# The weights' low part: an ACT negation and an accumulating DMA in place of DVE's subtraction

## Chip, cores and metric

One core of one Trainium2 chip runs the kernel. The metric is the device time of one execution in microseconds, the median of several runs. The work is in float32; the large products are done as float32r matmuls on split operands (below).

## The reference

Two transformer-like blocks are applied to 512 tokens of 1024 features. Cut to the dense products, which take most of the time:

```python
def first_block(x, p, ...):
    h = rms_norm(x, norm1_g)
    z = h @ w_in                     # 1024 -> 2304 columns, for four mixers
    x = x + concat(mixers(z)) @ w_out
    hf = causal_dwconv(rms_norm(x, norm2_g) @ w_up, ...)
    gt, val = split(hf)
    x = x + (gelu(gt) * val) @ w_down          # d_ff = 2816
    x = x + (p @ w_pe) * sigmoid(rms_norm(x, norm3_g) @ w_pg)
    return rms_norm(x, final_g)

def hybrid_layer(x, ...):            # the second block: two of these
    proj = (_rms(x) * norm1_g) @ w_in          # attention, RWKV, retention, gates
    mixed = g0 * (attention @ w_attn_o) + g1 * (rwkv @ w_rwkv_o) + g2 * (retention @ w_ret_o)
    x = x + mixed @ w_out
    h2 = _rms(x) * norm2_g
    return x + (silu(h2 @ w_ffn_gate) * (h2 @ w_ffn_up)) @ w_ffn_down    # d_ff = 2816
```

## The kernel before

Features lie on the 128 partitions and the 512 tokens along the free axis, so an activation is 8 tiles of 128 x 512. The weights come from DRAM in chunks of 128 x 1024 (512 KB): one output tile of 128 columns with its 8 k tiles of 128. There are 400 chunks: 138 of w_in (18 in the first block, 60 in each layer of the second), 44 of w_up, 24 of w_down, 24 of w_out, 8 of w_pg, 2 of w_pe, and in the two layers 88 of the gate and up weights, 48 of w_ffn_down, and 8 each of w_rwkv_o, w_attn_o and w_ret_o. The down products have 22 k tiles, in chunks of 8, 7 and 7.

Full precision comes from splitting. Each activation x is a pair (xh, xl) of float32r tiles whose sum is x, and each weight chunk is made into such a pair on the chip. `fetch` (L111) has SP load the raw chunk into one of three wraw buffers. `chunk` (L117) then lets ACT cast it to float32r (whi, L125), and DVE subtract that from the raw chunk (wlo, L126); whi and wlo have two buffers each. `mac` (L129) adds three products for every k tile, in this order, and PE works through its instructions in their order:

```python
self.nc.tensor.matmul(ps, hi[:, c], xh, start=first and k == 0, stop=False)          # L135
self.nc.tensor.matmul(ps, hi[:, c], xl, start=False, stop=False)                     # L136
self.nc.tensor.matmul(ps, lo[:, c], xh, start=False, stop=last and k == n - 1)       # L137
```

So a tile is 24 matmuls of 128 x 512, and wlo is wanted by the third of them. whi is free again when L136 of the last k tile has read it.

The stages follow each other: the first block's mixers, its w_up and w_down products (`ffn1`), the gate with w_pg; then for each of two layers the RWKV mixer, attention and retention, `combine` (L1319, which holds a chunk of w_attn_o and one of w_ret_o at once and uses each for two output tiles), w_out, and `ffn2` (L1342: gate and up tiles in turn, with DVE's L1350 and L1354, ACT's L1351 and the split L165, POOL's L1352; then the down product). In the mixers, dense tiles wait in a queue and are let in between the steps of the recurrences. POOL has some 280 instructions, single additions and multiplications such as L220 (the sum of squares for the norms) and L1352, and issues no DMA. SP issues nearly all of the DMAs.

The order of each engine's instructions comes from a scheduler that takes dependencies and priorities; fetch, cast and subtraction are raised by 300 places. On an engine the instructions run strictly in that order, and an instruction that waits holds up all that are behind it.

Of the kernel before, what the change touches and what calls it, by code (L numbers as in the profile page):

```python
# [10 lines left out]
F32 = mybir.dt.float32  # L11
F32R = mybir.dt.float32r
I32 = mybir.dt.int32
U8 = mybir.dt.uint8
AF = mybir.ActivationFunctionType
ALU = mybir.AluOpType
# [4 lines left out]
P = 128  # L21
# [4 lines left out]
EPS = 1e-6  # L26
# [8 lines left out]
class Kern:  # L35
# [9 lines left out]
    # Dense tiles that nothing waits for yet are kept in a queue; the mixers let  # L45
    # some of them in between their own steps, so that the tensor engine has work.
# [64 lines left out]
    def fetch(self, src):  # L111
        raw = self.tile(self.wp, [P, 1024], "wraw", bufs=3)
        with self.tc.high_priority(offset=300):
            self.nc.sync.dma_start(raw[:, :src.shape[-1]], src)
        return raw

    def chunk(self, src):  # L117
        """One chunk of a weight: its float32 values, and their two parts."""
        nc = self.nc
        n = src.shape[-1]  # L120
        raw = self.early.popleft() if self.early else self.fetch(src)
        hi = self.tile(self.wp, [P, 1024], "whi", F32R)
        lo = self.tile(self.wp, [P, 1024], "wlo", F32R)
        with self.tc.high_priority(offset=300):
            nc.scalar.copy(hi[:, :n], raw[:, :n])  # L125
            nc.vector.tensor_tensor(lo[:, :n], raw[:, :n], hi[:, :n].bitcast(F32), ALU.subtract)  # L126
        return hi, lo

    def mac(self, ps, w, xs, first, last):  # L129
        """ps += w.T @ x over the k tiles in xs, in three passes."""  # L130
        hi, lo = w
        n = len(xs)
        for k, (xh, xl) in enumerate(xs):
            c = slice(k * P, (k + 1) * P)
            self.nc.tensor.matmul(ps, hi[:, c], xh, start=first and k == 0, stop=False)  # L135
            self.nc.tensor.matmul(ps, hi[:, c], xl, start=False, stop=False)  # L136
            self.nc.tensor.matmul(ps, lo[:, c], xh, start=False, stop=last and k == n - 1)  # L137

    def dense(self, wname, m, xs, kcuts=None):
        """M tile m of a weight applied to the k tiles xs (pairs of parts)."""  # L140
        src = self.io[wname]
        ps = self.tile(self.mm, [P, 512], "mm")
        kcuts = kcuts or [len(xs)]
        k0 = 0
        for i, kn in enumerate(kcuts):
            w = self.chunk(src[m, :, k0 * P:(k0 + kn) * P])
            self.mac(ps, w, xs[k0:k0 + kn], i == 0, i == len(kcuts) - 1)
            k0 += kn
        return ps

    def dense2(self, wname, xs, use):
        """A weight with 4 k tiles: two M tiles to a chunk; use(m, psum)."""
        src = self.io[wname]
        for j in range(src.shape[0]):
            hi, lo = self.chunk(src[j])
            for i in range(2):
                ps = self.tile(self.mm, [P, 512], "mm")
                o = slice(i * 512, (i + 1) * 512)
                self.mac(ps, (hi[:, o], lo[:, o]), xs, True, True)
                use(2 * j + i, ps)  # L160

    def split_into(self, hi, lo, src, scale=1.0):
        """Two float32r parts of src * scale: hi + lo is exact."""
# [13 lines left out]
    def rsqrt(self, v, n):  # L177
        """v ** -0.5 for a small [128, n] tile of positive values."""
# [12 lines left out]
    def bcast(self, col):  # L191
        """[128 tokens, 4] -> PSUM [128, 512]: each token's value down a column."""
# [5 lines left out]
    def bcast_heads(self, col):  # L198
        """[128 tokens, 4 blocks x 2 heads] -> PSUM [2 x 64 features, 512 tokens]."""
# [7 lines left out]
    def token_sum(self, acc, ps, col):  # L207
        """Sum over features of acc into column col + 4 b of ps."""
# [16 lines left out]
    def norm_scale(self, acc):  # L225
        """The broadcast 1 / rms of the tokens, as an SBUF tile."""
# [32 lines left out]
    def mixers1(self, c2, x, xg, rb, pe):  # L259
# [19 lines left out]
        # small parameters  # L279
# [16 lines left out]
        # columns, the longest mixer's first  # L296
# [30 lines left out]
        # p @ w_pe, halved for the gate that comes later  # L327
# [29 lines left out]
        # the order of the k tiles on the host: d, a, b, c  # L357
# [50 lines left out]
    def rglru_consts(self, tp):  # L408
        nc, V = self.nc, self.vec
        # 2 softplus(-lam): e = exp(-|lam|), log1p(e) by the series of atanh  # L410
# [18 lines left out]
        # softplus(-lam) = max(-lam, 0) + 2 acc;  sp = twice that  # L429
# [73 lines left out]
    def hgrn2(self, zq, zf, zig, lvm, tp, yp):  # L503
        nc, V = self.nc, self.vec
        # lower bound: a softmax over the one layer, less its own first row
# [24 lines left out]
        # masked scores [s, t], one level of block size after another  # L530
        # (heads of one parity, a pair of windows: one PSUM bank)
# [57 lines left out]
        # values and decayed keys by token  # L589
# [10 lines left out]
        # states at the starts of the windows, block diagonal over pairs of heads  # L600
# [39 lines left out]
    def head_rms(self, dst, src, nh, tp, xi=None, xi2=None):  # L640
        """dst = src / rms over the last axis of [128, nh, 64] (src in PSUM); of src * xi, where given."""
# [13 lines left out]
    def ffn1(self, x, acc, xg, pe, xs_p):  # L655
# [28 lines left out]
        # the gate, and the two norms that follow it  # L684
# [3 lines left out]
        with tc.tile_pool(name="f1g", bufs=2) as gp:  # L688
# [14 lines left out]
            # y = a / rms(x4) with a = x4 * final_g; with v and w the means of the squares of  # L703
            # x4 and a, the norm of y on top comes to a * (w + EPS * (v + EPS)) ** -0.5
# [42 lines left out]
    def rwkv(self, c):  # L747
# [21 lines left out]
        # halves of parameters that go with tanh  # L769
# [33 lines left out]
        for p in range(4):  # L803
# [3 lines left out]
            # decays  # L807
# [13 lines left out]
            # in-context rate  # L821
# [4 lines left out]
            # keys  # L826
# [13 lines left out]
            # b, scaled; the order of the two halves of a chunk turns with its parity  # L840
# [8 lines left out]
            # bonus  # L849
# [6 lines left out]
            # values by token  # L856
# [6 lines left out]
            # scores  # L863
# [10 lines left out]
            # keys as they stand at the end of the chunk  # L874
# [6 lines left out]
    def rwkv_inverse(self, SC, kp):  # L881
        """The transposed inverses of I - A (64 x 64) in place of the A of SC."""
# [24 lines left out]
        # rows of the first diagonal block, for the block below it  # L907
# [28 lines left out]
    def rwkv_chain(self, SC, AR, BK, UV, end, gd, g2, kp):  # L936
# [29 lines left out]
        def ahead(c):  # L966
            """What a chunk needs apart from the state: decayed keys by token, products with the values."""
# [97 lines left out]
    def evac(self, dst, ps, scale=1.0):  # L1065
        """dst = ps * the tokens' 1 / rms (* scale)."""
# [42 lines left out]
    def att_proj(self, ap):  # L1109
# [10 lines left out]
        # keys and values  # L1120
# [17 lines left out]
        # queries: tile g has head g (of the first key head) over head 4 + g  # L1138
# [66 lines left out]
    def ret_proj(self, rp, rt):  # L1205
        """Queues the columns of the retention, and what is done to them one by one."""
# [48 lines left out]
    def retention(self, rp, op, q, k, vt, sg, cn):  # L1255
        nc, l = self.nc, self.l
        # the queries, keys and values, where the queue still has any
# [61 lines left out]
    def combine(self, oa, oc, mp):  # L1319
        """The gated sum of the three branches (twice it, halved in the split)."""  # L1320
# [56 lines left out]
def _w(a, per=1, cols=None, rows=None):  # L1377
    """[K, M] -> chunks [M tiles / per, 128, per * K tiles * 128], contiguous for a partition."""
# [13 lines left out]
def _col(v):  # L1392
    """[n * 128] -> [128, n]"""
    return np.ascontiguousarray(v.reshape(-1, P).T)


def _constants():
# [19 lines left out]
    # rotary angles and decays of the retention  # L1417
# [101 lines left out]
```

## Time and profile before

| | |
|---|---|
| median of 3 runs | 2668.3 us (2667.89 to 2669.66) |
| span of the profiled execution, from its first to its last instruction | 2666.0 us |
| what the median has beyond that span | 2.3 us |
| mean granted TensorE clock | 0.985 |
| busy: DVE, ACT, POOL | 1491.5, 893.7, 378.5 us |
| DRAM read, written | 244.42 MB, 31.72 MB |

The busy times are those of one execution, and an engine's share is an average over stages that differ. A time in a row of waits is the idle time of the engine at the left until the one at the right released it. Line numbers are those of the kernel before; in the changed kernel the lines of `mac` and all that is behind it stand two lower down (L135 becomes L137, L1352 becomes L1354).

### The profile page before, as it was taken

How to read it: one execution, taken by the hardware profiler on the slowest of the kernel's cores; microseconds unless marked ns; L12 is line 12 of the kernel's file. 1: busy time of each engine (PE TensorE's matmuls, PEld its weight loads, DVE VectorE, ACT ScalarE, POOL GpSimd, SP SyncE). 2: the span in 40 equal slices, each digit the busy share in tenths (PEclk: the TensorE clock that was granted, in tenths of full speed). 3: DMA queues.
4: the chain of work that ended last, by engine and by line, in shares of the span. 5: the costliest groups of instructions: out<-in, count | busy, mean ns of one | idle time of the engine just before them, and what ended most of it. 6: DMA issues, size and time to landing. Idle time of an engine off the chain costs nothing. (4 is left out here: it accounts for less than half of the span.)

```text
span 2666.0 us, 33302 instructions
## 1 busy us (share of the span) xinstructions
PE 2579.1 (97%) x13104; PEld 2052.8 (77%) x13104; DVE 1491.5 (56%) x2546; ACT 893.7 (34%) x1342; POOL 378.5 (14%) x277
## 2 busy tenths in 40 slices
PE   8989999999998999999999999998999999999999
PEld 6767888887776877677788887767877677788887
DVE  8775666336788455565443333788455565444322
ACT  4343444225332333522322222322333423332221
POOL 2111111013120001005311101120000004211100
PEclk9999999999999999999999999999999999999999
DMA  4132223334223143226422334223152226422332
GB/s 148 64 103 85 98 95 95 93 104 139 87 91 107 60 154 95 70 87 206 137 95 97 99 123 127 83 80 107 43 174 88 79 72 213 143 95 95 99 114 96
DMA packets 99502, 282.51 MB, mean 106 GB/s; under 512 B 13201, under 2 KB 14225, under 8 KB 99217
## 3 DMA queue, kind: packets, MB, share of 16 engines
q1 hardware_dynamic: 97616, 277.52, 31.8%
q10 hardware_dynamic: 1728, 2.87, 0.3%
q8 instruction: 103, 1.69, 0.3%
q14 instruction: 55, 0.44, 0.1%
HBM read 244.42 MB, written 31.72 MB: 104 GB/s over the span
## 5 line engine op out<-in xcount | busy, mean ns | idle before, releaser
L125 ACT CAST whi<-wraw 128x1024 fp32r<-128x1024 f32 (+1 forms) x400 | 414.6, 1037 | 1110.1 <-PE mm L136 735.1
L126 DVE TENSOR_TENSOR wlo<-wraw,whi 128x1024 fp32r<-128x1024 f32 (+1 forms) x400 | 491.9, 1230 | 246.6 <-ACT whi L125 237.1
L1352 POOL TENSOR_TENSOR fg<-fg,rb 128x512 f32<-128x512 f32 x44 | 78.3, 1780 | 396.1 <-ACT fg L1351 396.1
L135 PE MATMUL mm<-x0h,whi 128*128 128x512 f32 x286 | 116.2, 407 | 8.1 <-ACT x0h L165 8.1
L220 POOL TENSOR_TENSOR acc<-acc,sq 128x512 f32<-128x512 f32 x49 | 77.8, 1587 | 325.9 <-ACT sq L219 325.9
L137 PE MATMUL mm<-x0h,wlo 128*128 128x512 f32 x286 | 114.1, 399 | 6.0 <-DVE wlo L126 5.7
L135 PE MATMUL mm<-x2h,whi 128*128 128x512 f32 x286 | 114.3, 400 | 2.2 <-ACT x2h L165 2.2
L136 PE MATMUL mm<-x0l,whi 128*128 128x512 f32 x286 | 113.7, 397 | 1.2 <-DVE x0l L169 1.2
L136 PE MATMUL mm<-x2l,whi 128*128 128x512 f32 x286 | 114.6, 401 | 0.0
L136 PE MATMUL mm<-x5l,whi 128*128 128x512 f32 x286 | 112.9, 395 | 1.6 <-DVE x5l L169 1.6
L135 PE MATMUL mm<-x3h,whi 128*128 128x512 f32 x286 | 113.9, 398 | 0.0
L137 PE MATMUL mm<-x1h,wlo 128*128 128x512 f32 x286 | 113.7, 398 | 0.0
L136 PE MATMUL mm<-x3l,whi 128*128 128x512 f32 x286 | 113.1, 395 | 0.7 <-DVE x3l L169 0.7
L137 PE MATMUL mm<-x2h,wlo 128*128 128x512 f32 x286 | 113.7, 398 | 0.0
L136 PE MATMUL mm<-x1l,whi 128*128 128x512 f32 x286 | 113.3, 396 | 0.3 <-DVE x1l L169 0.3
L1354 DVE TENSOR_TENSOR fg<-fg,mm 128x512 f32<-128x512 f32 x44 | 30.3, 688 | 148.8 <-PE mm L137 148.8
L135 PE MATMUL mm<-x5h,whi 128*128 128x512 f32 x286 | 113.4, 397 | 0.0
L137 PE MATMUL mm<-x6h,wlo 128*128 128x512 f32 x286 | 113.3, 396 | 0.0
L135 PE MATMUL mm<-x6h,whi 128*128 128x512 f32 x286 | 113.3, 396 | 0.0
L135 PE MATMUL mm<-x7h,whi 128*128 128x512 f32 x286 | 113.2, 396 | 0.0
L137 PE MATMUL mm<-x7h,wlo 128*128 128x512 f32 x286 | 113.1, 396 | 0.0
L135 PE MATMUL mm<-x1h,whi 128*128 128x512 f32 x286 | 113.1, 395 | 0.0
(757 smaller groups left out, 6132.5 us busy)
## 6 DMA issues: line engine op xcount, KB each, us to landing
wraw<-in_w_in_dram SPq DMA_DIRECT2D x138, 512.0 KB, 3.5
wraw<-in_w_ffn_dram SPq DMA_DIRECT2D x88, 512.0 KB, 3.4
wraw<-in_w_up_dram SPq DMA_DIRECT2D x44, 512.0 KB, 3.3
wraw<-in_w_ffn_down_dram SPq DMA_DIRECT2D x32, 448.0 KB, 3.4
wraw<-in_w_out_dram SPq DMA_DIRECT2D x24, 512.0 KB, 3.5
gates<-gt SPq DMA_DIRECT2D x48, 256.0 KB, 2.1
cg<-gates SPq DMA_DIRECT2D x32, 256.0 KB, 3.8
gt<-xres SPq DMA_DIRECT2D x32, 256.0 KB, 3.3
```

The source lines that it names most:

```text
L125: nc.scalar.copy(hi[:, :n], raw[:, :n])
L126: nc.vector.tensor_tensor(lo[:, :n], raw[:, :n], hi[:, :n].bitcast(F32), ALU.subtract)
L135: self.nc.tensor.matmul(ps, hi[:, c], xh, start=first and k == 0, stop=False)
L136: self.nc.tensor.matmul(ps, hi[:, c], xl, start=False, stop=False)
L137: self.nc.tensor.matmul(ps, lo[:, c], xh, start=False, stop=last and k == n - 1)
L220: (eng or nc.gpsimd).tensor_tensor(acc, acc, s, ALU.add)
L1352: nc.gpsimd.tensor_tensor(g, g, rb, ALU.mult)
L1354: nc.vector.tensor_tensor(g, g, ps, ALU.mult)
```

## The change

`chunk` no longer lets DVE subtract. ACT writes the negated high part into wlo, from whi, right after the cast. Then a DMA issued on POOL's queue reads the weight chunk from DRAM a second time and adds it to what wlo holds, so that wlo is w - whi as before. The raw chunk is read by the cast alone. wraw has two buffers instead of three, wlo three instead of two; whi keeps two. What is computed is the same. All else in the diff is the removal of comments, left out here:

```diff
     def fetch(self, src):
-        raw = self.tile(self.wp, [P, 1024], "wraw", bufs=3)
+        raw = self.tile(self.wp, [P, 1024], "wraw", bufs=2)
         with self.tc.high_priority(offset=300):
             self.nc.sync.dma_start(raw[:, :src.shape[-1]], src)
         return raw
...
         raw = self.early.popleft() if self.early else self.fetch(src)
         hi = self.tile(self.wp, [P, 1024], "whi", F32R)
-        lo = self.tile(self.wp, [P, 1024], "wlo", F32R)
+        lo = self.tile(self.wp, [P, 1024], "wlo", F32R, bufs=3)
         with self.tc.high_priority(offset=300):
             nc.scalar.copy(hi[:, :n], raw[:, :n])
-            nc.vector.tensor_tensor(lo[:, :n], raw[:, :n], hi[:, :n].bitcast(F32), ALU.subtract)
+            nc.scalar.activation(lo[:, :n], hi[:, :n].bitcast(F32), AF.Copy, scale=-1.0)
+            nc.gpsimd.dma_start(lo[:, :n], src, accum_op=ALU.add)
         return hi, lo
```

Two places show how the scheduler sets the new instructions. The first is ACT's order in `ffn2` of the first layer, at the second to fourth gate and up tiles. whi and wlo are a chunk's two parts, wraw its raw copy, fg the gate tile, h0h and so on the high parts of the hidden tiles; the number behind a name tells its buffers apart. Before:

```order
L125 CAST whi_1852_10291<-wraw_1851_10289 128x1024
L165 ACTIVATE h0h_1843_10249<-fg_1838_10213 128x512
L125 CAST whi_1858_10327<-wraw_1857_10325 128x1024
L1351 ACTIVATE fg_1849_10284<-fg_1849_10284 128x512
L125 CAST whi_1863_10362<-wraw_1862_10360 128x1024
L165 ACTIVATE h1h_1854_10320<-fg_1849_10284 128x512
```

And of the change:

```order
L126 CAST whi_1852_10478<-wraw_1851_10476 128x1024
L167 ACTIVATE h0h_1843_10435<-fg_1838_10398 128x512
L127 ACTIVATE wlo_1853_10479<-whi_1852_10478 128x1024
L126 CAST whi_1858_10515<-wraw_1857_10513 128x1024
L1353 ACTIVATE fg_1849_10471<-fg_1849_10471 128x512
L127 ACTIVATE wlo_1859_10516<-whi_1858_10515 128x1024
L126 CAST whi_1863_10551<-wraw_1862_10549 128x1024
L167 ACTIVATE h1h_1854_10508<-fg_1849_10471 128x512
L127 ACTIVATE wlo_1864_10552<-whi_1863_10551 128x1024
```

The negation (L127) of a chunk does not follow its cast at once here: the split of the hidden tile or the silu stands between. Over the whole kernel 177 of the 400 negations follow their cast directly, 215 have one other instruction between, 8 have two.

The second place is POOL's order in the same stage, from the first gate tile on. Before, POOL has only the multiplication of the gate tile by rb, the tokens' norm:

```order
L1352 TENSOR_TENSOR fg_1838_10213<-fg_1838_10213,rb_1832_10169 128x512
L1352 TENSOR_TENSOR fg_1849_10284<-fg_1849_10284,rb_1832_10169 128x512
L1352 TENSOR_TENSOR fg_1860_10355<-fg_1860_10355,rb_1832_10169 128x512
L1352 TENSOR_TENSOR fg_1871_10426<-fg_1871_10426,rb_1832_10169 128x512
L1352 TENSOR_TENSOR fg_1882_10497<-fg_1882_10497,rb_1832_10169 128x512
```

And of the change:

```order
L1354 TENSOR_TENSOR fg_1849_10471<-fg_1849_10471,rb_1832_10353 128x512
L128 DMA wlo_1859_10516<-in_w_ffn_20_dram 128x1024
L128 DMA wlo_1864_10552<-in_w_ffn_20_dram 128x1024
L1354 TENSOR_TENSOR fg_1860_10544<-fg_1860_10544,rb_1832_10353 128x512
L128 DMA wlo_1870_10589<-in_w_ffn_20_dram 128x1024
L128 DMA wlo_1875_10625<-in_w_ffn_20_dram 128x1024
L1354 TENSOR_TENSOR fg_1871_10617<-fg_1871_10617,rb_1832_10353 128x512
L128 DMA wlo_1881_10662<-in_w_ffn_20_dram 128x1024
L128 DMA wlo_1886_10698<-in_w_ffn_20_dram 128x1024
```

Two DMAs stand between one multiplication and the next, so every second DMA is issued behind a multiplication. In `ffn1` POOL's multiplication L674 and in w_out the additions L220 stand among the DMAs in the same way. On PE the order of a tile's 24 matmuls is as before.

## Rows read from the trace of the kernel before

**Rows 1.** The page: busy time, share of the span and instructions of each engine.
```profile
PE 2579.1 (97%) x13104; PEld 2052.8 (77%) x13104; DVE 1491.5 (56%) x2546; ACT 893.7 (34%) x1342; POOL 378.5 (14%) x277
```
**Rows 2.** Waits of PE: line, releaser: us in total, times, longest.
```profile
PE ps L917 <- DVE iA L910: 9.8, 2, 5.1
...
PE mm L137 <- DVE wlo L126: 7.3, 7, 2.2
PE ps L852 <- DVE t L850: 6.3, 8, 1.1
PE ps L1308 <- DVE t L653: 3.6, 8, 0.9
PE ps L635 <- DVE hot L653: 3.4, 1, 3.4
PE ps L447 <- DVE t L444: 3.2, 1, 3.2
PE ps L976 <- DVE SC L934: 2.6, 4, 0.9
```
**Rows 3.** Groups by line and shape: count | busy us, mean ns | idle before, releasers.
```profile
L126 DVE TENSOR_TENSOR wlo<-wraw,whi 128x1024 fp32r<-128x1024 f32 x352 | 439.5, 1249 | 151.2 <-ACT whi L125 143.2
L125 ACT CAST whi<-wraw 128x1024 fp32r<-128x1024 f32 x352 | 369.2, 1049 | 932.3 <-PE mm L136 613.2 <-issue 316.7 <-ACT iQ L921 0.9
...
L220 POOL TENSOR_TENSOR acc<-acc,sq 128x512 f32<-128x512 f32 x49 | 77.8, 1587 | 325.9 <-ACT sq L219 325.9
...
L126 DVE TENSOR_TENSOR wlo<-wraw,whi 128x896 fp32r<-128x896 f32 x48 | 52.4, 1092 | 95.4 <-ACT whi L125 93.9
...
L669 ACT ACTIVATE fc<-fe,pv 128x512 f32<-128x512 f32 x44 | 35.8, 814 | 11.4 <-DVE fe L667 11.4
```
**Rows 4.** Timeline of `ffn2`, first layer: start, duration (us), instruction, [idle before].
```profile
1310.14 0.39 PE L135 MATMUL mm<-x0h,whi 128*128 128x512 f32 x1
1310.15 1.05 ACT L125 CAST whi<-wraw 128x1024 fp32r<-128x1024 f32 x1 [3.83 <-PE mm L136]
...
1310.36 0.39 PE L136 MATMUL mm<-x0l,whi 128*128 128x512 f32 x1
1310.59 0.39 PE L137 MATMUL mm<-x0h,wlo 128*128 128x512 f32 x1
...
1311.11 0.62 ACT L1351 ACTIVATE fg<-fg 128x512 f32<-128x512 f32 x1
1311.24 1.23 DVE L126 TENSOR_TENSOR wlo<-wraw,whi 128x1024 fp32r<-128x1024 f32 x1 [0.21 <-ACT whi L125]
...
1311.81 1.80 POOL L1352 TENSOR_TENSOR fg<-fg,rb 128x512 f32<-128x512 f32 x1 [8.22 <-ACT fg L1351]
...
1315.58 0.39 PE L135 MATMUL mm<-x0h,whi 128*128 128x512 f32 x1
...
1316.03 0.39 PE L137 MATMUL mm<-x0h,wlo 128*128 128x512 f32 x1
```
**Rows 5.** DMA: a queue's packets, MB and share of 16 engines; issues, KB, us to landing.
```profile
q1 hardware_dynamic: 97616, 277.52, 31.8%
...
wraw<-in_w_in_dram SPq DMA_DIRECT2D x138, 512.0 KB, 3.5
...
wraw<-in_w_up_dram SPq DMA_DIRECT2D x44, 512.0 KB, 3.3
...
rsw<-rq SPq DMA_DIRECT2D x16, 128.0 KB, 4.2
```
**Rows 6.** Timeline of PE at the second layer's norm before `ffn2`.
```profile
2299.18 1.05 PE L210 MATMUL ps<-ones,acc 128*128 128x1 f32 x8 [1.26 <-POOL acc L220]
...
2302.06 0.63 PE L135 MATMUL mm<-x6h,whi 128*128 128x512 f32 x1
2302.48 0.63 PE L136 MATMUL mm<-x6l,whi 128*128 128x512 f32 x1
```
**Rows 7.** Windows: length, busy us of each engine (count), granted clock, DMA share, GB/s.
```profile
2310.00:2500.00 190.00, 190.00 (x840) 157.34 (x839) 77.86 (x88) 55.82 (x70) 30.66 (x17) 1.00 0.30 96
...
840.00:850.00 10.00, 3.56 (x12) 2.61 (x13) 9.91 (x8) 2.19 (x3) 0.00 (x0) 0.67 0.36 113
```

## The prediction

> **What bounds the kernel now.** I read the page's busy shares first, then PE's list of waits, then the timeline of one dense tile, and last the DMA issues. The reader is to see in the busy row that PE works 97% of the span: 2579 of 2666 us [rows 1]. Only 87 us are idle, so nothing taken off another engine can win more than that. PE's own list of waits [rows 2] shows how little of the 87 is owed to DVE: the subtraction that the change removes (wlo, L126) held PE for 7.3 us in seven waits, and the six largest waits on other DVE work come to 9.8 + 6.3 + 3.6 + 3.4 + 3.2 + 2.6 = 28.9 us. DVE is busy for 56% and the subtraction is 439.5 + 52.4 us of that [rows 3], but DVE is not what PE waits for. So the question is not what DVE saves. It is whether the low part still arrives before PE asks for it.
>
> **How much time the low part has.** The timeline of the second block's gate and up tiles [rows 4] shows the cycle. Matmuls start 0.227 us apart, and a tile is 24 of them: 1310.14 to 1315.58 is 5.44 us. At 1310.15 ACT starts a cast, released by the last use of the other whi buffer. That chunk is wanted one tile later: its first wlo matmul (the third of the tile) starts at 1316.03. DVE's subtraction ends at 1311.24 + 1.23 = 1312.47, so there are 3.56 us to spare. With two whi buffers the cast cannot start earlier, whatever wlo has, so this is the whole allowance.
>
> After the change the cast ends at 1311.20, and ACT's negation takes its place: same engine, shape and output type as the cast, so 1.05 us [rows 3], to 1312.3 with 0.05 for each hand-over. The DMA then has 1316.03 - 1312.3 = 3.7 us from issue to landing. That is the allowance A0 where nothing stands between. In 223 of the 400 chunks ACT's new order has another instruction between cast and negation (one in 215, two in 8; none in 177). In this stage it is the silu or the split of the hidden tile, 0.62 us [rows 4]. POOL has one order too: in every second chunk its multiplication L1352 stands ahead of the DMA. It runs until 1311.81 + 1.80 = 1313.61 [rows 4], and the allowance there is 1316.03 - 1313.61 = 2.42 us.
>
> If the DMA takes A, PE stalls A minus the allowance once for two tiles, because the cast of chunk n+2 hangs on the end of chunk n and two such chains alternate. Of chains with unequal allowances the longer sets the pace. So the price per chunk is (A - allowance) / 2.
>
> **The price of the accumulating DMA.** No DMA of the trace accumulates, and none is issued by POOL, so I bound it. Low end: the plain load of the same tile from the same DRAM, 3.3 us at its best stage and 3.5 at its most frequent [rows 5]. High end: the rotary swap, which reads and writes SBUF, 128 KB in 4.2 us [rows 5]. The 16 engines' share of queue 1, 31.8% of 2666 us for 277.52 MB [rows 5], is 3.06 us a MB, or 1.6 us for a 512 KB tile, which leaves 1.8 us of a load that don't grow with size. The swap's other 2.4 us, times four for 512 KB, plus 1.8 give 11.4 us. I take the value nearest the load, since tile, source and row length are the same: 3.5, plus 1.6 since the old content must be read as well, plus 0.5 for sharing the engines with the load of a later raw tile: **A = 5.6 us**. Two passes of 1.6 us more for each of 400 tiles are 1280 us on top of the 848, some 70% of the longer span: the engines still fit.
>
> By the Trainium skill (DMA: Bandwidth & Descriptors, section on the anatomy of one DMA on the SWDGE path) a DMA of this kind costs about 2.0 us plus its bytes at 436 GB/s, and by Collectives: The Full Stack (section on the bandwidth ceiling) an add reads two sources and runs at half rate; together an estimate of 2.0 + 2 x 1.2 = 4.4 us, by which the time would be about 2890. The load's 3.5 us against the first rule's 3.2 agrees roughly; no row here shows the second.
>
> **The sum, at A = 5.6.**
> - 88 gate and up chunks of the second block: (5.6 - 2.42) / 2 = 1.59, 140 us.
> - 44 w_up chunks: ACT's convolution start (0.81 [rows 3]) between cast and negation: (5.6 - 3.7 + 0.81) / 2 = 1.35, 59 us.
> - 72 chunks of the down products (24, 21, 21 matmuls): the tile is 0.45 us shorter on average, cast, negation and DMA together about 0.4 shorter: (1.9 + 0.05) / 2 = 0.98, 71 us.
> - 24 w_out chunks: one ACT instruction (0.63) and half of POOL's 1.59 us addition [rows 3] in the way: (1.9 + 0.63 + 0.8) / 2 = 1.67, 40 us. 8 w_pg chunks, bare: 0.95, 8 us.
> - 16 chunks of combine: attention and retention weights are live together, so the first of a pair is freed only half a chunk (12 x 0.227 = 2.72 us) before its successor is wanted: 1.9 + 2.72 = 4.6 for each of 8 pairs, 37 us.
> - 148 chunks in the mixers (w_in, w_pe, w_rwkv_o): other PE work lies between many of them, others come in bursts, so I take half of the bare price, 0.48: 71 us.
>
> Together 426 us. Against it stands the relief of DVE. I take 10 us: the 7.3 of L126, and a little of the chains in the inverse [rows 2]. The rest of DVE's 492 us saved is beside PE's work and costs or gains nothing. ACT's 400 negations, 420 us, raise it from 34% to about 43% of the longer span, beside PE as well, apart from the terms above. wraw's third buffer is dropped at no cost: the raw tile is now freed by the cast, 5.44 us x 2 before the next use of its buffer, and a load takes 3.5. SP only loses a wait. If A is long, PE's stall gives the loads more time still.
>
> 2666 + 416 = 3082 us of span. The median of the runs is 2668.3, 2.3 above the profiled span, so the forecast is **3084 us**. At the low end (3.3 to 3.4 us) only the stages with ACT or POOL in the way pay: 39 + 9 + 12 + 18 - 10 = 68, about 2737. At 7.5 us the sum is 426 + 224 + 15 + 70 = 735, about 3390. At 11.4 us it is some 1360, about 4030.
>
> **The rivals.**
> - *Hidden after all (not slower).* If A stays under 2.4 us in the gate and up stage and under 3.7 elsewhere, no chunk stalls, and what is left is DVE's relief: at most the 36 us of the waits added up [rows 2]. That gives 2632 to 2668. For it: the DMA engines are idle two thirds of the time. Against it: every plain load of that size already takes 3.3 us or more, and this one moves more. It decides at A = 2.4. 6%.
> - *A small price.* A between 3.3 and 4.2: 2737 to 2860. 12%.
> - *A dear accumulation.* Read, add and write of SBUF go at the swap's price per byte, A from 7.5 to 11.4: 3390 to 4030. For it: the only rows that read SBUF and write it. Against it: they come four in a row, with 32 partitions each. 14%.
> - *The clock falls too.* After idle PE the matmuls start 0.43 us apart, not 0.227 [rows 6], and the stretch with PE busy for 3.56 of 10 us has a granted clock of 0.67 (half is 1.2 GHz), where the busy ones have 1.00 [rows 7]. If a third of the 236 dense chunks ran at 0.43, each would take 10.3 us in place of 7.0: 78 x 3.3 = 257 us more, 3340. Against it: the stalls expected are 1 to 3 us, shorter than the idle spells before the rows that are slow. The Trainium skill (TensorE: Matmul & The Clock Gate, section on HAM oscillation) tells of a kernel that lost its clock at each wait for a DMA between groups of matmuls; a fall after a wait is what this trace shows too [rows 6]. 8%.
>
> **How the numbers follow.** The forecast's case (A from 4.2 to 7.5, 2860 to 3390) has 60%. The range 2740 to 3620 leaves out the hidden case, the edge of the small price, and two thirds of the dear case, some 16 to 18 in 100. A measurement here tells 0.2% from no change (5 us). Faster by more: 0.04, most of the hidden case. Same: 0.03. Slower: 0.93.
>
> **What would show it.** PE's first wlo matmul of a tile should head PE's waits, released by the accumulating DMA, a gap once in one or two tiles, 1 to 3 us long in the gate and up stage. wlo's DMA should take 5 to 6 us from issue to landing; PE's busy time stays near 2580 while the span grows; DVE falls to about 1000 us and ACT rises to about 1310. PE's gaps without a DMA as releaser would make the prediction wrong, as would a DMA of under 3.7 us with the span unchanged, or a granted clock well under 0.95 in the dense stages.

## The result, and the profile after

The changed kernel takes **3237.1 us** (median of 4 runs, 3218.5 to 3254.8) against 2668.1 for the kernel before: ratio 1.213, interval 1.209 to 1.218. The prediction was 3084, with a range of 2740 to 3620: the sign and the range hold, the likeliest value is 153 us short. The profiled execution of after took 3239.2 us, its span is 3237.1, 571.1 more than before.

The page of the changed kernel first: busy time and share of each engine, then two queues with packets, MB and their share of the 16 DMA engines (q0 carries POOL's DMAs).

```profile
PE 2755.5 (85%) x13104; PEld 2117.6 (65%) x13104; DVE 1047.0 (32%) x2146; ACT 1284.3 (40%) x1742; POOL 664.7 (21%) x677
...
q0 software_dynamic: 57600, 206.60, 38.9%
q1 hardware_dynamic: 97616, 277.52, 26.8%
```

DVE fell from 56% to 32% and nothing was won by it. PE, the bound of before [rows 1], is idle for 481.6 us in place of 86.9, and its busy time has grown by 176 though it does the same matmuls. Two things are to be explained: a wait and a slower PE. The wait stands in PE's list (us in total, times, longest):

```profile
PE mm L139 <- DMA wlo<-in_w_ffn_dram: 100.5, 62, 3.6
PE mm L139 <- DMA wlo<-in_w_in_dram: 99.8, 50, 6.7
PE mm L139 <- DMA wlo<-in_w_ffn_down_dram: 58.3, 31, 3.1
PE mm L139 <- DMA wlo<-in_w_up_dram: 54.6, 28, 4.0
PE mm L139 <- DMA wlo<-in_w_out_dram: 38.5, 16, 4.5
```

All rows on wlo's DMA add up to 434 us in 219 waits, where DVE's subtraction had 7.3 in seven [rows 2]. The other rows of the list fell together from 74.5 to 40.6. The DMA issues (count, KB, median us from issue to landing) show the cause:

```profile
wraw<-in_w_in_dram SPq DMA_DIRECT2D x138, 512.0 KB, 3.6
wlo<-in_w_in_dram POOLq DMA_DIRECT2D x138, 512.0 KB, 6.0
wraw<-in_w_ffn_dram SPq DMA_DIRECT2D x88, 512.0 KB, 3.5
wlo<-in_w_ffn_dram POOLq DMA_DIRECT2D x88, 512.0 KB, 5.5
```

The raw loads land as before [rows 5]; the accumulating DMA of the same tile takes 2 to 2.5 us more. The timeline of `ffn2` in the first layer, the stage of [rows 4], shows how that becomes a gap in every second tile:

```profile
1609.35 1.05 ACT L126 CAST whi<-wraw 128x1024 fp32r<-128x1024 f32 x1 [5.51 <-PE mm L138]
...
1609.84 0.40 PE L139 MATMUL mm<-x0h,wlo 128*128 128x512 f32 x1
...
1610.91 1.04 ACT L127 ACTIVATE wlo<-whi 128x1024 fp32r<-128x1024 f32 x1
...
1612.25 0.87 POOL L128 DMA_DIRECT2D wlo<-in_w_ffn_dram  x1 [7.19 <-ACT wlo L127]
...
1614.82 1.05 ACT L126 CAST whi<-wraw 128x1024 fp32r<-128x1024 f32 x1 [2.87 <-PE mm L138]
...
1616.31 1.04 ACT L127 ACTIVATE wlo<-whi 128x1024 fp32r<-128x1024 f32 x1
1616.48 1.26 POOL L1354 TENSOR_TENSOR fg<-fg,rb 128x512 f32<-128x512 f32 x1 [3.37 <-ACT fg L1353]
...
1617.69 0.50 PE L139 MATMUL mm<-x0h,wlo 128*128 128x512 f32 x1 [2.23 <-DMA wlo<-in_w_ffn_dram]
1617.69 0.86 POOL L128 DMA_DIRECT2D wlo<-in_w_ffn_dram  x1
```

The cast at 1609.35 is released by the last use of the other whi buffer. Negation, POOL and 5.44 us of DMA follow, and PE stands for 2.23 us at 1617.69. The tile at 1609.84 did not wait: its chunk was filled while PE stood in the gap before, so one gap serves two chunks. (The row has 62 waits for 88 chunks, not 44: some second tiles wait a little too.)

The slower PE is in the rows of matmuls. The same stage, a little later:

```profile
1672.81 0.50 PE L139 MATMUL mm<-x0h,wlo 128*128 128x512 f32 x1 [2.40 <-DMA wlo<-in_w_ffn_dram]
1673.14 0.40 PE L137 MATMUL mm<-x1h,whi 128*128 128x512 f32 x1
...
1674.77 0.63 PE L137 MATMUL mm<-x3h,whi 128*128 128x512 f32 x1
1675.19 0.63 PE L138 MATMUL mm<-x3l,whi 128*128 128x512 f32 x1
...
1677.96 0.39 PE L139 MATMUL mm<-x5h,wlo 128*128 128x512 f32 x1
1678.19 0.39 PE L137 MATMUL mm<-x6h,whi 128*128 128x512 f32 x1
```

After a gap of 2.40 us the matmuls first start 0.23 us apart, then for 3 us 0.43 apart (the lower of the two clock levels, as in [rows 6]), then 0.23 again. The mean granted clock fell from 0.985 to 0.948. With levels of 1.2 and 2.4 GHz that is 2 x 0.015 x 2666 = 80 us at the lower level before, and 2 x 0.052 x 3237 = 337 after. Half of the difference, 128 us, is the most that this can cost, as if PE had matmuls to run all through those stretches. Three windows of after (columns as in [rows 7]) show that it is not alike everywhere: w_down 0.92, the first combine with w_out 0.91, the first gate and up 0.96, where before had 1.00 in each. The last line is before's window of the first combine with w_out.

```profile
548.00:714.80 166.80, 139.55 (x535) 107.90 (x534) 18.79 (x26) 59.49 (x68) 29.73 (x31) 0.92 0.68 140
...
1382.90:1521.10 138.20, 110.74 (x482) 86.37 (x478) 40.70 (x80) 47.58 (x58) 44.38 (x40) 0.91 0.77 195
1521.10:1839.90 318.80, 262.46 (x1068) 206.12 (x1068) 49.83 (x81) 116.21 (x138) 71.31 (x71) 0.96 0.69 152
...
1166.20:1270.60 104.40, 101.39 (x497) 80.72 (x496) 62.74 (x111) 31.10 (x41) 36.44 (x22) 1.00 0.53 179
```

So of the 571 us 569 are: 427 more waiting for wlo (434 - 7), 34 less for all else, up to 128 of clock, and a rest of at least 48 us, PE's busy time beyond the clock's. (The other 2 us are idle time that the list of waits doesn't name.) The rest is a remainder and wasn't measured by itself; it fits the edges of the 219 gaps, some 0.22 us each: the first matmul after a gap holds PE for 0.50 in place of 0.39, and the one before it isn't overlapped. By stage (lengths between the first fetches of each weight, for w_pg from its first fetch to its last; the last 5 to 6 us of the span count with the mixers; waits are PE's on wlo):

| stage | before | after | more | waits | predicted stall |
|---|---|---|---|---|---|
| gate and up, both layers | 487.6 | 630.3 | 142.7 | 100.5 | 140 |
| w_up | 246.5 | 312.4 | 65.9 | 54.6 | 59 |
| down products, three | 390.6 | 515.8 | 125.2 | 84.0 | 71 |
| w_pg | 39.7 | 51.4 | 11.7 | 11.9 | 8 |
| combine, and w_out | 206.2 | 277.0 | 70.8 | 74.6 | 77 |
| mixers | 1295.4 | 1450.2 | 154.8 | 108.5 | 71 |

(The first block's w_out lies in the lengths of the last row, its waits and its prediction in the row above.)

### The profile page after: what moved, and what is told of

Its sections match the earlier page's. It is cut to its first block, busy times and chain, and to the rows that moved or that the text cites. A ratio compares the mean times of both kernels' runs of the same rounds, so it can differ in the third digit from the quotient of the medians.

```text
span 3237.1 us, 34252 instructions
## 1 busy us (share of the span) xinstructions
PE 2755.5 (85%) x13104; PEld 2117.6 (65%) x13104; DVE 1047.0 (32%) x2146; ACT 1284.3 (40%) x1742; POOL 664.7 (21%) x677
## 4 chain that ended last, share of the span: by engine, by line
PE 33%; issue 26%; DMA 24%; ACT 7%; POOL 5%; DVE 4%; SPq 0%; POOLq 0%; ACTq 0%; DVEq 0%
PE mm L139 10%; PE mm L137 9%; PE mm L138 9%; DMA wlo<-in_w_ffn_dram 7%; DMA wlo<-in_w_in_dram 5%; ACT wlo L127 3%; ACT whi L126 3%; DMA wlo<-in_w_up_dram 2%; POOL wlo L128 2%; DMA wlo<-in_w_out_dram 2%; DMA wlo<-in_w_ffn_down_dram 2%; DMA wlo<-in_w_down_dram 1%; DMA wlo<-in_w_ret_o_dram 1%; DMA wlo<-in_w_attn_o_dram 1%; DMA wlo<-in_w_pg_dram 1%
## 5 line engine op out<-in xcount | busy, mean ns | idle before, releaser
L127 ACT ACTIVATE wlo<-whi 128x1024 fp32r<-128x1024 f32 (+1 forms) x400 | 414.8, 1037 | 5.8
L139 PE MATMUL mm<-x0h,wlo 128*128 128x512 f32 x286 | 136.6, 478 | 274.6 <-DMA wlo<-in_w_ffn_dram 100.5
L139 PEld LDWEIGHTS mm<-x0h,wlo 128*128 128x128 f32 x286 | 55.7, 195 | 351.3 <-DMA wlo<-in_w_ffn_dram 130.0
L128 POOL DMA_DIRECT2D wlo<-in_w_in_dram x138 | 120.4, 873 | 764.0 <-ACT wlo L127 690.7
L128 POOL DMA_DIRECT2D wlo<-in_w_ffn_dram x88 | 76.0, 863 | 326.1 <-ACT wlo L127 317.6
L137 PE MATMUL mm<-x2h,whi 128*128 128x512 f32 x286 | 122.4, 428 | 0.4 <-ACT x2h L167 0.4
L139 PE MATMUL mm<-x3h,wlo 128*128 128x512 f32 x286 | 117.0, 409 | 0.0
L137 PE MATMUL mm<-x4h,whi 128*128 128x512 f32 x286 | 115.8, 405 | 0.0
L138 PE MATMUL mm<-x4l,whi 128*128 128x512 f32 x286 | 114.4, 400 | 0.0
L139 PE MATMUL mm<-x4h,wlo 128*128 128x512 f32 x286 | 113.9, 398 | 0.0
```

Of the source, the lines that this page charges most:

```text
L127: nc.scalar.activation(lo[:, :n], hi[:, :n].bitcast(F32), AF.Copy, scale=-1.0)
L128: nc.gpsimd.dma_start(lo[:, :n], src, accum_op=ALU.add)
```

## The experiments

Theory 1 is the prediction's: the low part of a chunk must be refilled within the turn of two buffers, and the DMA's time to landing does not fit. Theory 2: the DMA engines or POOL's queue can't carry 400 more transfers. Beside these: ACT's second pass, the buffer counts, or POOL's order might cost the time. The expectations number the rivals anew each time: theory 2 here is theory 3 in those on the third whi buffer, on the order of the products and on the delay without a DMA.

**Is it the DMA at all?** DVE adds the raw chunk to ACT's negation; all else is as changed.

```diff
-            nc.gpsimd.dma_start(lo[:, :n], src, accum_op=ALU.add)
+            nc.vector.tensor_tensor(lo[:, :n], raw[:, :n], lo[:, :n].bitcast(F32), ALU.add)
```

> As the changed kernel, but DVE adds the raw chunk to the negated high part, so that no DMA accumulates; ACT's 400 negations and the new numbers of buffers stay. Theory 1 (the accumulating DMA's latency, against an allowance that the two whi buffers set): cast 1.05, negation 1.05 and DVE's 1.23 us fit into the 5.9 us that a low part has, PE stalls no more on wlo, the PE busy time goes back to about 2580 us and the clock to about 0.985: 2655 to 2685 us. Theory 2 (ACT's second pass over each chunk, or a raw chunk less): a good part of the 570 us stays, over 2800 us.

Measured: 2678.1 us, ratio 1.0021 (1.0011 to 1.0032). PE's row for wlo in this kernel:

```profile
PE mm L139 <- DVE wlo L128: 22.1, 18, 3.0
```

By this ratio ACT's 400 negations, two wraw and three wlo buffers cost some 6 us together (3 to 9); the other 563 or so of the 569 us need the DMA.

**The buffers' turn, first way.** A third whi buffer, paid for with one of wraw's.

```diff
-        raw = self.tile(self.wp, [P, 1024], "wraw", bufs=2)
+        raw = self.tile(self.wp, [P, 1024], "wraw", bufs=1)
...
-        hi = self.tile(self.wp, [P, 1024], "whi", F32R)
+        hi = self.tile(self.wp, [P, 1024], "whi", F32R, bufs=3)
```

> As the changed kernel, with three whi buffers and, for the room, one wraw buffer. Theory 1: a cast may now start a whole tile (5.44 us) earlier, which is more than the 2 to 3 us by which the DMA is late; the stalls on wlo go nearly all, 2665 to 2750 us (the single raw buffer makes load 3.5 + cast 1.05 follow each other, 4.7 us of 5.44, so a little may come back in the mixers). Theory 3 (the DMA engines' or POOL's throughput is the limit, since every byte is loaded twice and the engines are busy for 66%): more buffers change little, over 3050 us.

Measured: 2755.3 us, ratio 1.0311 (1.0293 to 1.0328), a little above what was expected. The queue of POOL's DMAs and the window of w_up in this kernel:

```profile
q0 software_dynamic: 57600, 206.60, 45.7%
```
```profile
217.30:461.80 244.50, 242.40 (x1070) 199.06 (x1069) 114.18 (x205) 147.28 (x180) 69.62 (x68) 1.00 0.88 190
```

w_up takes 244.5 us, as short as before (246.5), with the DMA engines at 0.88. After needs 312.4 for it, with them at 0.69. The same transfers, packed closer, cost nothing: theory 2 falls. What is left lies in the first layer's mixers (569.5 against 547.5) and in combine with w_out (250.7 against 206.2); PE's waits on wlo are still 60 us in all.

**The buffers' turn, second way.** PE takes all high products of a tile first, then the low ones, so wlo is wanted 16 matmuls later.

```diff
             self.nc.tensor.matmul(ps, hi[:, c], xh, start=first and k == 0, stop=False)
             self.nc.tensor.matmul(ps, hi[:, c], xl, start=False, stop=False)
+        for k, (xh, xl) in enumerate(xs):
+            c = slice(k * P, (k + 1) * P)
             self.nc.tensor.matmul(ps, lo[:, c], xh, start=False, stop=last and k == n - 1)
```

> As the changed kernel, but mac runs the 16 products with the high part first and the 8 with the low part behind them. Theory 1: the low part is wanted by the seventeenth matmul, 3.2 us later in the tile, and whi is free seven or eight matmuls (1.6 us) earlier, so the allowance grows by 4.8 us and no dense tile stalls: 2640 to 2680 us, with DVE's relief visible if there is any. Theory 3: over 3050 us. Theory 4 (part of the loss is the clock, and the clock falls from something else than the stalls): PE's busy time stays over 2700 us although the stalls are gone.

Measured: 2763.3 us, ratio 1.0344 (1.0325 to 1.0364): the direction held, the size didn't. The dense stages are back (w_up 243.1, gate and up 249.1 and 244.0), but not combine with w_out, whose windows in this kernel are:

```profile
1177.00:1322.10 145.10, 117.97 (x512) 92.59 (x510) 42.86 (x82) 50.50 (x60) 45.48 (x41) 0.89 0.71 184
...
2229.70:2369.20 139.50, 115.82 (x513) 91.35 (x512) 40.22 (x81) 50.51 (x60) 40.30 (x37) 0.91 0.74 193
```

They are 78 us longer than the 206.2 of before, most of the 92 that this kernel loses by its ratio. `combine` holds two chunks at once and uses each for two tiles, so the buffers turn at another pace there, as the prediction's own term for it says; the next run tests that.

**That leftover undone.** The same order, and DVE's subtraction again in combine and in the second block's w_out: 32 of the 400 chunks.

```diff
+            if dma:
                 nc.scalar.activation(lo[:, :n], hi[:, :n].bitcast(F32), AF.Copy, scale=-1.0)
                 nc.gpsimd.dma_start(lo[:, :n], src, accum_op=ALU.add)
+            else:
+                nc.vector.tensor_tensor(lo[:, :n], raw[:, :n], hi[:, :n].bitcast(F32), ALU.subtract)
...
-            ca = self.chunk(io[f"w_attn_o_2{l}"][j])
+            ca = self.chunk(io[f"w_attn_o_2{l}"][j], False)
```

> As the kernel with the high products first, but in combine and in the second block's w_out DVE subtracts as before, so that 32 of the 400 chunks have no accumulating DMA. Of that kernel's 90 us over the kernel before, 79 lie in these two stages. If they come from the low parts' DMA there (two chunks live at once in combine), they go: 2665 to 2695 us. If they come from the order of the products, or from the DMA traffic around, most of them stay: over 2730 us.

Measured: 2681.0 us, ratio 1.0048 (1.0030 to 1.0065). With 368 accumulating DMAs and DVE at 1087.6 us the kernel is within 13 us of before. So the DMAs can be hidden; and with them hidden, 404 us less of DVE win nothing.

**Does the order alone do something?** The kernel before, with the order of products of the last two.

> The kernel before, with the 16 products of the high part first and the 8 of the low part behind them; nothing else changed. A control: PE waits for wlo only 7.3 us there, so the order by itself can win little: 2655 to 2675 us. If the order of the products costs PE time by itself (weights loaded, PSUM, or w_out and combine), it is slower than 2690 us.

Measured: 2681.9 us, ratio 1.0052 (1.0037 to 1.0067), 7 us over what was expected, and the same as with the DMAs. Its largest wait is on the inverse (L919, 17.5 us, against 9.8 [rows 2]).

**The size of the latency.** The DMA only overwrites wlo: the addition is left out, the bytes read from DRAM are the same.

```diff
-            nc.gpsimd.dma_start(lo[:, :n], src, accum_op=ALU.add)
+            nc.gpsimd.dma_start(lo[:, :n], src)
```

> As the changed kernel, but POOL's DMA overwrites wlo instead of adding to it, so the low part is the weight itself and the addition is left out. It tells what of the 5.5 to 6 us is the accumulation and what is the issue from POOL. If the second read of wlo is the price, the DMA takes about 4.0 to 4.4 us from issue to landing and the time falls to 2800 to 2950 us; if the software-made descriptors and the issue from POOL are, it stays over 5.2 us and over 3100 us. The engines' share of queue 0 falls from 38.9% to about 27 to 30% in the first case.

Measured: 2924.0 us, ratio 1.0945 (1.0910 to 1.0980). DMA issues and queue in this kernel:

```profile
wlo<-in_w_ffn_dram POOLq DMA_DIRECT2D x88, 512.0 KB, 4.2
```
```profile
q0 software_dynamic: 57600, 206.60, 25.0%
```
The DMA lands 1.3 us sooner, and the waits on wlo fall from 434 to 212: 0.56 us a chunk, near the 1.3 / 2 that the price (A - allowance) / 2 gives. The add costs engine time: 0.389 x 3237 / 400 = 3.15 us a chunk, against 0.250 x 2920 / 400 = 1.83 without it, 1.72 times. (The share of 25.0% is a little under what was expected.) By the Trainium skill (Collectives: The Full Stack, section on the bandwidth ceiling) an add reads two sources and runs at half rate, which would be 2 times; the 1.72 has the direction and falls short of the size. The Trainium skill's rule for such a DMA without an add (DMA: Bandwidth & Descriptors, section on the anatomy of one DMA on the SWDGE path) would give an estimate of 3.2 us; the trace has 4.2, and the prediction's estimate of 4.4 for the accumulating one was too low as well, against 5.5.

**The latency without a DMA.** After the negation ACT copies wlo (1.06 us on average), DVE multiplies it by one (0.79), and POOL adds the raw chunk (2.43): a delay of some 4.3 us with no second read of the weights.

```diff
-            nc.gpsimd.dma_start(lo[:, :n], src, accum_op=ALU.add)
+            nc.scalar.activation(lo[:, :n], lo[:, :n].bitcast(F32), AF.Copy, scale=1.0)
+            nc.vector.tensor_scalar(lo[:, :n], lo[:, :n].bitcast(F32), 1.0, None, ALU.mult)
+            nc.gpsimd.tensor_tensor(lo[:, :n], lo[:, :n].bitcast(F32), raw[:, :n], ALU.add)
```

> As the changed kernel, with its buffers, cast and negation, but no DMA adds: ACT copies the negated part onto itself (1.05 us), DVE multiplies it by 1 (about 0.7 to 1.2 us), POOL adds the raw chunk (about 3.4 us, twice the 1.78 of its 512-wide multiplication). Together some 5.5 to 6 us between negation and low part, as long as the DMA takes, without a byte of extra DMA traffic. Theory 1 (only the delay counts): 3100 to 3350 us, PE's waits on wlo some 350 to 550 us in all, now released by POOL, and the clock falls to about 0.95 as well. Theory 3 (the doubled DMA traffic, or something else that only the DMA does, is the loss): under 2900 us.

Measured: 3071.3 us, ratio 1.1508 (1.1482 to 1.1535), just under the first range; the waits, 250 us, are under theirs too. The delay came out shorter than the 5.5 to 6 us meant.

```profile
PE mm L141 <- POOL wlo L130: 250.5, 191, 5.7
```

The clock is 0.965. A delay without the DMA, with the DMA traffic of before, stalls PE and slows its clock. (Besides the delay, this kernel has ACT at 55% and POOL at 42%, and frees the raw chunk only behind POOL's addition; PE's list has no wait on the raw loads.)

**A smaller DMA.** Two accumulating DMAs of half the columns.

```diff
+            for o in (0, 512):
+                nc.gpsimd.dma_start(lo[:, o:min(o + 512, n)], src[:, o:min(o + 512, n)], accum_op=ALU.add)
```

> As the changed kernel, with the accumulating DMA cut into two halves of 512 columns. PE wants the second half 12 matmuls (2.7 us) after the first. Theory 1: the first half has half the transfer time (3.15 us of engine time a chunk becomes 1.6), lands about 1.5 us earlier, and the second is issued 0.87 us later, within its 2.7: the stalls on wlo fall from 434 us to 120 to 250, the time to 2850 to 3000 us, and the clock rises more than in proportion. If the fixed part of the DMA is nearly all of its 5.5 us, the time stays over 3150 us.

Measured: 3030.5 us, ratio 1.1356 (1.1338 to 1.1373): less won than expected.

```profile
wraw<-in_w_ffn_dram SPq DMA_DIRECT2D x88, 512.0 KB, 4.3
wlo<-in_w_ffn_dram POOLq DMA_DIRECT2D x176, 256.0 KB, 5.3
```

The 5.3 is the median over both halves. Taken by the order of issue, the first half of a gate or up chunk lands after 4.7 us (median) and the second, issued 0.6 us later, after 5.7. So the half that PE asks for first is 0.8 us sooner than a whole (5.5), not the 1.5 expected, and the waits on wlo fall from 434 to 256. Two DMAs are in flight at once, and the raw load slows from 3.5 to 4.3. Which part of the 4.7 is fixed and which is sharing isn't told apart by this.

**The POOL term.** In `ffn2` the gate tile's multiplication goes from POOL to DVE.

```diff
-                nc.gpsimd.tensor_tensor(g, g, rb, ALU.mult)
+                nc.vector.tensor_tensor(g, g, rb, ALU.mult)
```

> The changed kernel with the gate tile's multiplication in ffn2 (L1354) moved from POOL to DVE, so that POOL's queue holds nothing but the accumulating DMAs there. Theory of the prediction's POOL term: the multiplication takes 1.3 us off the allowance of every second chunk, 88 x 1.3 / 2 = 57 us, so about 3180. What the changed kernel's timeline shows instead: the DMA is issued only 0.35 us later than the negation's end in the chunk that has it, because the silu ahead of the negation has already used up most of that time; if the longer chain of the two sets the pace, 88 x 0.35 = 31 us at most, 3205 to 3237. If POOL's queue is what makes the DMA late: under 3150.

Measured: 3239.4 us, ratio 1.2139 (1.2111 to 1.2167): no difference to the changed kernel. The wait on the gate and up weights is 98.8 us against 100.5. The prediction's POOL term, 57 us by the expectation, isn't there. The timeline of after above says why: without the multiplication the DMA starts 0.30 us after the negation's end (1611.95 to 1612.25), with it 0.34 (1617.35 to 1617.69). The silu ahead of the negation had delayed it as long, and the multiplication now takes 1.26 us, not the 1.80 of [rows 4].

**The raw buffer.** The kernel before with two wraw and three wlo.

> The kernel before with only the numbers of buffers changed as the change has them: wraw two, wlo three; DVE's subtraction kept. Prediction: the third raw buffer is dropped at no cost: 2663 to 2673. But DVE's subtraction still reads the raw chunk here and frees it some 1.3 us later than a cast alone would, so a little more wait is possible. If the raw buffers are short: over 2690, with PE or ACT waiting on the raw loads.

Measured: 2666.4 us, ratio 0.9992 (0.9983 to 1.0001). The third raw buffer is worth nothing, as the prediction had it.

**Which buffer binds?** The counts of whi and wlo exchanged.

```diff
-        hi = self.tile(self.wp, [P, 1024], "whi", F32R)
-        lo = self.tile(self.wp, [P, 1024], "wlo", F32R, bufs=3)
+        hi = self.tile(self.wp, [P, 1024], "whi", F32R, bufs=3)
+        lo = self.tile(self.wp, [P, 1024], "wlo", F32R, bufs=2)
```

> The changed kernel with the buffers exchanged: whi three, wlo two. Theory 1 (latency against the turn of the buffers): the cast is off the chain, but the negation now waits for the wlo that the chunk before last frees, 0.23 us later than whi. The chain is shorter by cast and hand-over less 0.23, some 0.9 us, so the gap of 2.25 us in two tiles falls to some 1.3, the waits on wlo from 434 to some 250, and the time to 2880 to 3000. If the clock falls only with the longer gaps, the time at half clock falls to that of the kernel whose DMA only overwrites (100 us). Theory 2 (engines or queue too slow for 400 more DMAs): still 3200 or over.

Measured: 3238.5 us, ratio 1.2126 (1.2105 to 1.2148): a miss, by theory 2's number. ACT's order of instructions in this kernel shows a reason that neither theory had:

```order
L1353 ACTIVATE fg_1904_10836<-fg_1904_10836 128x512
L126 CAST whi_1924_10953<-wraw_1923_10951 128x1024
L127 ACTIVATE wlo_1919_10917<-whi_1918_10916 128x1024
L167 ACTIVATE h6h_1909_10873<-fg_1904_10836 128x512
L126 CAST whi_1929_10989<-wraw_1928_10987 128x1024
L127 ACTIVATE wlo_1925_10954<-whi_1924_10953 128x1024
```

The cast that stands ahead of a negation is the next chunk's (whi_1924 before the negation of whi_1918), in 386 of 400 chunks. Both are released by the same tile, whi 0.23 us before wlo, so the cast's 1.05 us is back in the chain. The trace shows that this is only part of the reason:

```profile
1606.28 1.05 ACT L126 CAST whi<-wraw 128x1024 fp32r<-128x1024 f32 x1 [5.33 <-issue]
...
1607.35 0.33 SPq L114 DMA_DIRECT2D wraw<-in_w_ffn_dram  x1
...
1608.59 0.85 POOL L128 DMA_DIRECT2D wlo<-in_w_ffn_dram  x1 [6.98 <-ACT wlo L127]
```
```profile
wlo<-in_w_ffn_dram POOLq DMA_DIRECT2D x88, 512.0 KB, 5.9
```

From the cast's start to the DMA's issue it is 2.31 us here (1606.28 to 1608.59) and 2.90 in after (1609.35 to 1612.25), so 0.6 us was won in spite of the order. The DMA takes 5.9 us to land in place of 5.5, and most of the 0.6 is gone.

**The order mended.** The last two products of a tile change places, so wlo comes free first, and 397 of 400 negations stand ahead of the next cast.

```diff
+            if k < n - 1:
+                self.nc.tensor.matmul(ps, hi[:, c], xl, start=False, stop=False)
-            self.nc.tensor.matmul(ps, hi[:, c], xl, start=False, stop=False)
-            self.nc.tensor.matmul(ps, lo[:, c], xh, start=False, stop=last and k == n - 1)
+            self.nc.tensor.matmul(ps, lo[:, c], xh, start=False, stop=False)
+        self.nc.tensor.matmul(ps, hi[:, c], xl, start=False, stop=last)
```

> The kernel with whi three and wlo two gained nothing (3238.5). In ACT's order there the cast of the next chunk stands ahead of the negation in 386 of 400 chunks, since whi comes free 0.23 us before wlo, so the cast's 1.05 us was back in the chain. Here only the last two products of a tile change places (the low product of the last k tile before hi times xl), so that wlo comes free first; now 397 of 400 negations stand ahead of the next cast. Buffers as there. Theory 1 (latency against the turn of the buffers, with ACT's order in the chain): the negation starts at the end of the tile, 0.23 us earlier than the cast did; landing 5.5 to 5.9 us; the gap in gate and up falls from 2.25 us in two tiles to 0.5 to 0.9, PE's waits on wlo from 434 to 160 to 220, and the time to 2820 to 2930. Rival: two wlo buffers or the traffic are what costs, not ACT's order: 3150 or over.

Measured: 3192.1 us, ratio 1.1928 (1.1885 to 1.1972): some 46 us won, far from what was expected. The timeline of `ffn2` and the DMA issues of this kernel:

```profile
1609.73 0.39 PE L137 MATMUL mm<-x0h,whi 128*128 128x512 f32 x1
1609.75 1.06 ACT L127 ACTIVATE wlo<-whi 128x1024 fp32r<-128x1024 f32 x1 [3.00 <-issue]
...
1612.82 0.50 PE L140 MATMUL mm<-x0h,wlo 128*128 128x512 f32 x1 [2.48 <-DMA wlo<-in_w_ffn_dram]
```
```profile
wraw<-in_w_ffn_dram SPq DMA_DIRECT2D x88, 512.0 KB, 6.6
wlo<-in_w_ffn_dram POOLq DMA_DIRECT2D x88, 512.0 KB, 7.1
```

The negation now starts with the next tile, 1609.75 beside 1609.73, as meant. But the time to landing grew from 5.5 to 7.1 us, and the raw load's from 3.5 to 6.6. In this kernel the cast follows the negation, so the freed raw buffer's load is issued about 0.7 us after the accumulating DMA (1606.25 and 1605.59, an earlier chunk), and the two run side by side. In after the load starts 1.8 us ahead (1602.39 and 1604.19). Both pairs, this kernel's first:

```profile
1605.59 0.88 POOL L128 DMA_DIRECT2D wlo<-in_w_ffn_dram  x1 [5.59 <-ACT wlo L127]
...
1606.25 0.33 SPq L114 DMA_DIRECT2D wraw<-in_w_ffn_dram  x1
```
```profile
1602.39 0.33 SPq L114 DMA_DIRECT2D wraw<-in_w_ffn_dram  x1
...
1604.19 0.86 POOL L128 DMA_DIRECT2D wlo<-in_w_ffn_dram  x1
```

The 1.6 us that the DMA takes longer ate most of the gain: PE's waits on wlo are 421 us, against 434. The amount of traffic does not bind, as the run with DMA engines at 0.88 showed; the landing goes with what runs beside the DMA. Three kernels stand in one line: with the load 1.8 us ahead the DMA lands after 5.5 us, with the load 1.2 us ahead (1607.35 and 1608.59, the kernel above) after 5.9, with the load 0.7 us behind after 7.1. That this overlap is the reason is read from these issue times; no run changes the distance of the two DMAs alone.

No version beats the kernel before. The nearest with the DMA is 0.5% behind (2681.0). Without it, other numbers of buffers are level (2666.4), DVE's addition is 0.2% behind and the order of the products 0.5%.

## Why the prediction was right, and where it fell short

- **What bounds the kernel.** Right. DVE was not what PE waited for: e7's 404 us less of DVE bought nothing.
- **The mechanism, and one gap for two tiles.** Right, by the timeline of after, and by the two ways of lengthening the turn (2755 and 2763).
- **A = 5.6 us.** Right: 5.5 to 6.1 for the four large stages (6.3 to 8.1 for w_out, w_pg, w_rwkv_o, w_attn_o and w_ret_o). The bounds, 3.3 and 11.4, were too far apart to give it; the choice of the nearest row did. Its parts were each a little off: the overwriting DMA takes 4.2, 0.7 over the load where the sum had 0.5 for sharing, and the addition 1.3 where it had 1.6.
- **The stalls, 426 us.** Measured 434. Of the terms, two were wrong and offset each other. Gate and up was 40 too high (140, measured 100): its allowance of 2.42 us counted POOL's multiplication in full. After shows DMA issue at 1612.25 and wlo wanted at 1617.69 - 2.23 = 1615.46, an allowance of 3.21, and (5.44 - 3.21) / 2 = 1.12 for 88 chunks is 98 (half of the gap of 2.23). The mixers were 37 too low (71, measured 108): half the bare price was taken for them, and 0.73 us a chunk came. That the total is within 2% is luck in so far as these two cancel.
- **The relief of 10 us.** PE's other waits fell by 34. How much of that is DVE's doing and how much is hidden behind PE's gaps isn't told apart.
- **What failed: the clock.** The forecast's sum has no term for it; it stood apart, as a rival with 8% and 257 us. It came on top of the stalls, with at most 128 us. The argument against it was that stalls of 1 to 3 us are shorter than the idle spells ahead of the slow rows [rows 6]. Those rows don't bear that out: the idle spell in them is 1.26 us, with 1.05 us of one-column matmuls behind it. In after the fall at 1674 follows a gap of 2.40 us. The prediction named a clock well under 0.95 in the dense stages as what would make it wrong: gate and up have 0.96 and 0.97, but w_down 0.92 and combine 0.90 to 0.91, so by its own sign it failed there. PE's busy time, which was to stay near 2580, is 2755.5.
- **Also missing:** the gaps' edges, 48 us. 426 - 10 + 128 + 48, with 8 more of stalls and 31 more of relief (34 + 7 of the old wait on wlo, against 10), is 569; 128 is the most for the clock and 48 what is then left.

The Trainium skill (TensorE: Matmul & The Clock Gate, section on HAM oscillation) tells of a kernel that lost its clock at every wait for a DMA. Here it was some of the waits: from 1601 to 1671 the gaps of 0.8 to 2.3 us left the granted clock at 1.00, and the one of 2.40 lowered it for 3 us. The length of a gap alone does not decide it. In the same stage of after a gap of 2.35 us has slow matmuls right behind it (0.43 apart), and one of 2.36 has none (0.24 apart):

```profile
1687.98 0.80 PE L139 MATMUL mm<-x0h,wlo 128*128 128x512 f32 x1 [2.35 <-DMA wlo<-in_w_ffn_dram]
1688.57 0.63 PE L137 MATMUL mm<-x1h,whi 128*128 128x512 f32 x1
1689.00 0.63 PE L138 MATMUL mm<-x1l,whi 128*128 128x512 f32 x1
...
1814.77 0.50 PE L139 MATMUL mm<-x0h,wlo 128*128 128x512 f32 x1 [2.36 <-DMA wlo<-in_w_ffn_dram]
1815.11 0.40 PE L137 MATMUL mm<-x1h,whi 128*128 128x512 f32 x1
1815.35 0.39 PE L138 MATMUL mm<-x1l,whi 128*128 128x512 f32 x1
```

## What to carry to other kernels

Ask of a moved step not how long its engine is busy but how long the buffer takes from free to full (every instruction and hand-over between, and the DMA's time to landing) and compare that with the time for which the other buffers of the same tile feed PE. If it is longer, PE stops for the difference though DVE, ACT and POOL are idle for 60% of the time or more, and the stops have a second price, here 176 us of slower PE on top of 434. When buffers are added, read the producer's instruction order too: the next chunk's work may stand ahead of what the new buffer set free.

## What the runs showed of the hardware

- An accumulating DMA of 512 KB, DRAM onto SBUF, from POOL's queue: 5.5 to 6.0 us to landing (medians of w_in, w_up, and gate and up), 3.15 us of the 16 engines, and 0.87 us of POOL to issue. Overwriting: 4.2 to 4.8 us and 1.83. With a raw load issued 0.7 us behind it: 7.1.
- The clock's loss does not follow the number or the sum of the waits alone. Time at the lower level, 2 x (1 - clock) x span:

| kernel | waits on wlo, us (times) | mean granted clock | us at the lower level |
|---|---|---|---|
| before | 7 (7) | 0.985 | 80 |
| changed | 434 (219) | 0.948 | 337 |
| delay without a DMA | 250 (191) | 0.965 | 215 |
| overwriting DMA | 212 (199) | 0.983 | 99 |
| high products first | 71 (27) | 0.977 | 127 |
| DVE adds | 22 (18) | 0.987 | 69 |

The overwriting DMA makes as many waits as the changed kernel, of 1.1 us on average, and costs hardly any clock (99 us against 80 before); 27 waits of 2.6 us on average, with the high products first, cost more (127). In these kernels few long waits are worse for it than many short ones. No length at which it begins can be read from them, as the two gaps of 2.35 and 2.36 us show.
